# A row-softmax with relative position bias: loads and stores alternating on one queue, in larger chunks, with a written-out order

## The chip, the cores and the metric

The kernel runs on one core of one Trainium2 chip. The metric is the device time of one execution in microseconds (us), as the median of several runs. All runs compared here are of the fast state, except one, which is marked. Times of the kernel before agree within about 0.1%. The sets of experiments ran on three chips, with the kernel before run anew in each set (medians of 1334.1 to 1334.5 us), so a few tenths of a microsecond between sets say nothing.

## The reference

For each of 16 matrices (2 batches, 8 heads) of 2112 x 2112 float32 logits, a bias that depends only on the clipped distance between row and column is added, and each row goes through a softmax:

```python
rel = clip(pos[:, None] - pos[None, :], -16, 16) + 16
logits = logits + rel_bias[:, rel]
logits = logits - logits.max(axis=-1, keepdims=True)
exp = np.exp(logits)
return exp / exp.sum(axis=-1, keepdims=True)
```

Input and output together are 571 MB. Every byte of the input is read once and every byte of the output written once, so this is mostly a copy with arithmetic on the way. (Neither kernel subtracts the row maximum.)

## The kernel before

VectorE, ScalarE, GpSimd and SyncE are engines of the core; the profile calls them DVE, ACT, POOL and SP. Here the last three issue transfers, each into a queue of its own, and the core's 16 DMA engines carry them out. PEclk in the tables belongs to an engine that is not used here.

A partition holds 33 consecutive rows of one head, so 128 partitions hold two heads. A chunk is 3 rows of every partition, 25,344 contiguous bytes per partition. A chunk is loaded, gets the bias added by VectorE in one instruction (`F` is a strip that holds the bias row once, read at a shifted offset for each row), goes through the exponential on ScalarE with the row sums as a by-product, is multiplied by the reciprocal on VectorE, and is stored from the same buffer.

```python
R = 3
io = ctx.enter_context(tc.tile_pool(name="io", bufs=7))
...
def load(c, eng):
    k, row, j, r = c
    L = io.tile([P, R * S], FP32, tag="L", name="L")
    eng.dma_start(out=L[:, 0 : r * S], in_=rows(logits, row, j, r))
    return L

NPRE = 2
pre = [load(c, nc.sync) for c in chunks[:NPRE]]
...
for n, c in enumerate(chunks):
    ...
    L = pre[n] if n < NPRE else load(c, nc.gpsimd)       # loads: GpSimd's queue
    ...
    nc.vector.tensor_tensor(out=L3, in0=L3, in1=F3, op=ALU.add)
    for i in range(r):
        x = L[:, i * S : (i + 1) * S]
        nc.scalar.activation(out=x, in_=x, func=EXP, accum_out=tot[:, i : i + 1])
    nc.vector.reciprocal(out=tot[:, 0:r], in_=tot[:, 0:r])
    for i in range(r):
        x = L[:, i * S : (i + 1) * S]
        nc.vector.tensor_scalar_mul(out=x, in0=x, scalar1=tot[:, i : i + 1])
    nc.sync.dma_start(out=rows(out, row, j, r), in_=L[:, 0 : r * S])   # stores: SyncE's queue
```

A scheduler decides in which order each engine runs these instructions. Loads (after the first two) are issued by GpSimd and stores by SyncE, so two DMA queues are at work.

The softmax here doesn't subtract the row's maximum and nothing guards it: scores larger than these inputs give would overflow.

Of the kernel before, what the change touches and what calls it, by code (L numbers as in the profile page):

```python
# [1 line left out]

# [4 lines left out]

FP32 = mybir.dt.float32
EXP = mybir.ActivationFunctionType.Exp
ALU = mybir.AluOpType  # L10


@with_exitstack
def kernel(
    ctx: ExitStack,
    tc: tile.TileContext,
    logits: bass.AP,
    rel_bias: bass.AP,
    out: bass.AP,
):  # L20




    nc = tc.nc
    P = 128
    B, H, S, S2 = logits.shape
    assert S == S2
    MR = 16
    W = 2 * MR + 1  # L30
    NB = S // W
    assert NB * W == S and 2 * NB == P and H % 2 == 0
    R = 3
    FW = S + W - 1

    const = ctx.enter_context(tc.tile_pool(name="const", bufs=1))
    fpool = ctx.enter_context(tc.tile_pool(name="fpool", bufs=2))
    io = ctx.enter_context(tc.tile_pool(name="io", bufs=7))
    small = ctx.enter_context(tc.tile_pool(name="small", bufs=8))

    chunks = []
    for k in range(H // 2):
        for b in range(B):
            last = k == H // 2 - 1 and b == B - 1
            sizes = [R] * (W // R)
            if last:
                sizes = sizes[:-1] + [1] * R
            j = 0
            for r in sizes:
                chunks.append((k, (b * H + 2 * k) * S, j, r))  # L50
                j += r
            assert j == W

    def rows(t, row, j, r):
        return bass.AP(
            tensor=t.tensor,
            offset=t.offset + (row + j) * S,
            ap=[[W * S, P], [1, r * S]],
        )

    def load(c, eng):
        k, row, j, r = c
        L = io.tile([P, R * S], FP32, tag="L", name="L")
        eng.dma_start(out=L[:, 0 : r * S], in_=rows(logits, row, j, r))  # L64
        return L

    NPRE = 2
    pre = [load(c, nc.sync) for c in chunks[:NPRE]]

    rbB = const.tile([P, H // 2, 2, W], FP32, tag="rbB")  # L70
    nc.scalar.dma_start(
        out=rbB,
        in_=bass.AP(tensor=rel_bias.tensor, offset=rel_bias.offset, ap=[[0, P], [1, H * W]]),
    )

    qm = const.tile([P, NB], FP32, tag="qm")
    for p0 in (0, NB):
        nc.gpsimd.iota(  # L78
            qm[p0 : p0 + NB],
            pattern=[[-1, NB]],  # L80
            base=0,
            channel_multiplier=1,
            allow_small_or_imprecise_dtypes=True,
        )
    eq = const.tile([P, NB], FP32, tag="eq")
    lt = const.tile([P, NB], FP32, tag="lt")
    gt = const.tile([P, NB], FP32, tag="gt")
    for m, op in ((eq, ALU.is_equal), (lt, ALU.is_gt), (gt, ALU.is_lt)):
        nc.vector.tensor_scalar(out=m, in0=qm, scalar1=0.0, scalar2=None, op0=op)  # L89
    rbP = const.tile([P, H // 2, W], FP32, tag="rbP")  # L90
    nc.vector.tensor_copy(out=rbP[0:NB], in_=rbB[0:NB, :, 0, :])  # L91
    nc.vector.tensor_copy(out=rbP[NB:P], in_=rbB[NB:P, :, 1, :])  # L92

    def bias_rows(k):

        F = fpool.tile([P, FW], FP32, tag="F", name="F")
        low = rbP[:, k, W - 1 : W]
        high = rbP[:, k, 0:1]
        rest = small.tile([P, NB], FP32, tag="rest", name="rest", bufs=2)
        nc.vector.tensor_scalar(out=rest, in0=lt, scalar1=low, scalar2=None, op0=ALU.mult)  # L100
        nc.vector.scalar_tensor_tensor(  # L101
            out=rest, in0=gt, scalar=high, in1=rest, op0=ALU.mult, op1=ALU.add
        )
        pitch = list(F.ap[0])[0]
        blocks = bass.AP(
            tensor=F.tensor, offset=F.offset + MR, ap=[[pitch, P], [W, NB], [1, W]]
        )
        rpitch = list(rbP.ap[0])[0]
        rev = bass.AP(
            tensor=rbP.tensor,  # L110
            offset=rbP.offset + k * W + W - 1,
            ap=[[rpitch, P], [0, NB], [-1, W]],
        )

        def wide(t):
            return bass.AP(
                tensor=t.tensor, offset=t.offset, ap=[[list(t.ap[0])[0], P], [1, NB], [0, W]]
            )

        nc.vector.tensor_tensor(out=blocks, in0=wide(eq), in1=rev, op=ALU.mult)  # L120
        nc.vector.tensor_tensor(out=blocks, in0=blocks, in1=wide(rest), op=ALU.add)  # L121
        nc.vector.tensor_copy(out=F[:, 0:MR], in_=low.to_broadcast([P, MR]))  # L122
        nc.vector.tensor_copy(out=F[:, FW - MR : FW], in_=high.to_broadcast([P, MR]))  # L123
        return F

    F, fk = None, None
    for n, c in enumerate(chunks):
        k, row, j, r = c
        if k != fk:
            F, fk = bias_rows(k), k  # L130
        L = pre[n] if n < NPRE else load(c, nc.gpsimd)
        pitch = list(L.ap[0])[0]
        L3 = bass.AP(tensor=L.tensor, offset=L.offset, ap=[[pitch, P], [S, r], [1, S]])

        F3 = bass.AP(
            tensor=F.tensor,
            offset=F.offset + W - 1 - j,
            ap=[[list(F.ap[0])[0], P], [-1, r], [1, S]],
        )
        nc.vector.tensor_tensor(out=L3, in0=L3, in1=F3, op=ALU.add)  # L140
        tot = small.tile([P, R], FP32, tag="tot", name="tot")
        for i in range(r):
            x = L[:, i * S : (i + 1) * S]
            nc.scalar.activation(out=x, in_=x, func=EXP, accum_out=tot[:, i : i + 1])  # L144
        nc.vector.reciprocal(out=tot[:, 0:r], in_=tot[:, 0:r])  # L145
        for i in range(r):
            x = L[:, i * S : (i + 1) * S]
            nc.vector.tensor_scalar_mul(out=x, in0=x, scalar1=tot[:, i : i + 1])  # L148
        nc.sync.dma_start(out=rows(out, row, j, r), in_=L[:, 0 : r * S])


# [1 line left out]
_INS = ['logits', 'rel_bias']  # L153
_OUTS = [((2, 8, 2112, 2112), 'float32')]


# [23 lines left out]
```

## Time and profile before

The median was 1334.06 us (1333.6 to 1334.38, three runs), the span of the profiled execution 1332.3 us.

| what | before |
|---|---|
| bytes moved | 571.19 MB |
| VectorE, ScalarE busy | 71%, 39% |
| DMA between 400 and 800 us | share 1.00, 432 GB/s |
| rbB landed, first add, first store issued | 17.9, 26.4, 57.0 us |

From the page of the kernel before: the span, one line of busy time, the two DMA rows over 40 slices, the packets, and the two queues with the share of the 16 DMA engines' time that their packets took.

```profile
span 1332.3 us, 1666 instructions
...
DVE 947.2 (71%) x473; ACT 524.9 (39%) x529; POOL 49.0 (4%) x94
...
DMA  9999999999999999999999999999999999999998
GB/s 392 415 402 432 432 435 431 434 431 434 431 434 430 434 431 433 432 432 434 432 434 430 434 432 433 432 434 431 433 434 432 432 432 434 431 432 432 433 428 372
DMA packets 26076, 571.19 MB, mean 429 GB/s; under 512 B 2896, under 2 KB 3024, under 8 KB 3024
...
q1 hardware_dynamic: 13248, 291.97, 51.0%
q0 software_dynamic: 12672, 278.99, 48.8%
```

The DMA engines are busy from end to end and everything else waits for them. Only the first three slices and the last two are below the plateau.

The table by stretches, for the kernel before: each line is a stretch, its length, the busy time of each engine, the clock, the DMA share and GB/s.

```profile
core 0: us, DVE busy (x) ACT busy (x) POOL busy (x), PEclk, DMA share, GB/s
30.00:110.00 80.00, 78.44 (x34) 47.59 (x48) 2.11 (x4) 1.00 0.99 415
110.00:190.00 80.00, 57.06 (x30) 33.30 (x33) 2.63 (x5) 1.00 1.00 431
190.00:270.00 80.00, 53.28 (x28) 32.13 (x34) 2.64 (x5) 1.00 1.01 433
270.00:400.00 130.00, 96.37 (x47) 51.05 (x51) 5.43 (x9) 1.00 1.00 433
400.00:800.00 400.00, 283.01 (x140) 157.11 (x160) 13.71 (x26) 1.00 1.00 432
```

After 110 us the kernel before runs at its plateau. Before that it loses rate. One cause is a microsecond in which nothing was queued; in a finer table of the same kernel (the same columns, two lines of it):

```profile
56.00:57.00 1.00, 1.00 (x2) 1.00 (x1) 0.00 (x0) 1.00 0.01 0
57.00:58.00 1.00, 1.00 (x1) 1.00 (x3) 0.00 (x0) 1.00 0.89 380
```

All seven buffers had been loaded and no store had been issued. The timeline of SyncE (start, length, what was issued) shows why:

```profile
start us, us, engine line op out<-in xcount [idle before <-releaser]
0.74 0.86 SPq L64 DMA_DIRECT2D L<-in_logits_dram  x2
57.02 57.79 SPq L149 DMA_DIRECT2D out_dram<-L  x7
```

The scheduler had VectorE run adds, from 26.4 to 53.2 us, before the scales that the first store needs. The start as a whole was late, since the bias table `rbB` shared the engines with the packets of two loading queues; VectorE's waits for the kernel before say so (total, count, longest):

```profile
DVE L L140 <- DMA L<-in_logits_dram: 346.6, 77, 8.2
DVE rbP L91 <- DMA rbB<-in_rel_bias_dram: 17.9, 1, 17.9
```

### The profile page before, as it was taken

The numbers are of one execution on the slowest core, as the hardware profiler recorded it, in microseconds if no ns is written. First come the engines' busy times: TensorE is split into PE (matmuls) and PEld (weight loads), VectorE is DVE, ScalarE is ACT, GpSimd is POOL, SyncE is SP. The second block draws the span as 40 slices with busy tenths as digits, with TensorE's granted clock in tenths as the row PEclk, the third lists the DMA queues.
The fourth block names the chain that finished last, engine by engine and source line by source line (L and its number), as shares of the span: only waits on it lengthen the run. The fifth ranks groups of instructions, "written<-read, shape, count | busy, mean of one in ns | idle before, by whom it ended". The sixth has DMA issues, their size and how long they took to land.

```text
span 1332.3 us, 1666 instructions
## 1 busy us (share of the span) xinstructions
DVE 947.2 (71%) x473; ACT 524.9 (39%) x529; POOL 49.0 (4%) x94
## 2 busy tenths in 40 slices
DVE  4997677669676677767966677766796677766773
ACT  0754334433344333443344333443334333443341
POOL 0000000000000000000000000000000000000000
DMA  9999999999999999999999999999999999999998
GB/s 392 415 402 432 432 435 431 434 431 434 431 434 430 434 431 433 432 432 434 432 434 430 434 432 433 432 434 431 433 434 432 432 432 434 431 432 432 433 428 372
DMA packets 26076, 571.19 MB, mean 429 GB/s; under 512 B 2896, under 2 KB 3024, under 8 KB 3024
## 3 DMA queue, kind: packets, MB, share of 16 engines
q1 hardware_dynamic: 13248, 291.97, 51.0%
q0 software_dynamic: 12672, 278.99, 48.8%
q10 hardware_dynamic: 144, 0.14, 0.0%
q14 instruction: 12, 0.10, 0.0%
HBM read 285.61 MB, written 285.47 MB: 429 GB/s over the span
## 4 chain that ended last, share of the span: by engine, by line
DMA 79%; DVE 11%; issue 7%; another core or an unknown queue 1%; ACT 0%; POOLq 0%; POOL 0%; ACTq 0%
DMA out_dram<-L 47%; DMA L<-in_logits_dram 30%; DVE L L148 6%; DVE L L140 4%; DMA rbB<-in_rel_bias_dram 1%; DVE F L121 0%; DVE F L120 0%; ACT L L144 0%; DVE tot L145 0%; POOLq L64 0%; POOL L L64 0%; DVE rest L100 0%; DVE rest L101 0%; DVE rbP L92 0%
## 5 line engine op out<-in xcount | busy, mean ns | idle before, releaser
L140 DVE TENSOR_TENSOR L<-L,F 128x6336 f32<-128x6336 f32 (+1 forms) x90 | 594.7, 6609 | 346.8 <-DMA L<-in_logits_dram 346.6
L144 ACT ACTIVATE L<-L 128x2112 f32<-128x2112 f32 x264 | 515.2, 1952 | 768.7 <-DVE L L140 756.5
L148 DVE TENSOR_SCALAR L<-L,tot 128x2112 f32<-128x2112 f32 x264 | 331.8, 1313 | 0.0
L64 POOL DMA_DIRECT2D L<-in_logits_dram x88 | 48.5, 551 | 1241.2 <-DMA out_dram<-L 1231.6
L144 ACT ACTIVATION_READ_ACCUMULATOR L<-L 128x1 f32 x264 | 49.2, 186 | 0.0
L145 DVE RECIPROCAL tot<-tot 128x3 f32<-128x3 f32 (+1 forms) x90 | 14.8, 167 | 0.9 <-ACT L L144 0.9
L91 DVE COPY rbP<-rbB 64x132 f32<-64x132 f32 x1 | 0.2, 223 | 17.9 <-DMA rbB<-in_rel_bias_dram 17.9
L121 DVE TENSOR_TENSOR F<-F,rest 128x2112 f32<-128x2112 f32 x4 | 9.4, 2344 | 0.0
L120 DVE TENSOR_TENSOR F<-eq,rbP 128x2112 f32<-128x2112 f32 x4 | 9.4, 2344 | 0.0
L144 ACT ACT_TABLE_LOAD x1 | 1.3, 1283 | 17.8 <-DMA L<-in_logits_dram 17.8
L101 DVE SCALAR_TENSOR_TENSOR rest<-gt,rbP,rest 128x64 f32<-128x64 f32 x4 | 1.0, 265 | 0.0
L100 DVE TENSOR_SCALAR rest<-lt,rbP 128x64 f32<-128x64 f32 x4 | 0.9, 240 | 0.0
L122 DVE COPY F<-rbP 128x16 f32<-128x16 f32 x4 | 0.7, 163 | 0.0
L123 DVE COPY F<-rbP 128x16 f32<-128x16 f32 x4 | 0.7, 167 | 0.0
L78 POOL IOTA qm<- 64x64 f32 x2 | 0.4, 176 | 0.4 <-PEq L175 0.4
L92 DVE COPY rbP<-rbB 64x132 f32<-64x132 f32 x1 | 0.2, 225 | 0.0
L89 DVE TENSOR_SCALAR lt<-qm 128x64 f32<-128x64 f32 x1 | 0.2, 186 | 0.0
L89 DVE TENSOR_SCALAR gt<-qm 128x64 f32<-128x64 f32 x1 | 0.2, 186 | 0.0
L89 DVE TENSOR_SCALAR eq<-qm 128x64 f32<-128x64 f32 x1 | 0.2, 185 | 0.0
L164 POOL MEMSET const-float32-0.0<- 128x1 f32 x1 | 0.1, 98 | 0.2 <-issue 0.2
L164 POOL MEMSET const-bfloat16-1.0<- 128x1 bf16 x1 | 0.1, 101 | 0.0
L164 POOL MEMSET const-float32-1.0<- 128x1 f32 x1 | 0.1, 98 | 0.0
(1 smaller groups left out, 0.1 us busy)
## 6 DMA issues: line engine op xcount, KB each, us to landing
out_dram<-L SPq DMA_DIRECT2D x87, 3168.0 KB, 38.2
L<-in_logits_dram POOLq DMA_DIRECT2D x85, 3168.0 KB, 25.7
L<-in_logits_dram SPq DMA_DIRECT2D x2, 3168.0 KB, 24.3
L<-in_logits_dram POOLq DMA_DIRECT2D x3, 1056.0 KB, 17.0
out_dram<-L SPq DMA_DIRECT2D x3, 1056.0 KB, 18.3
rbB<-in_rel_bias_dram ACTq DMA_DIRECT2D x1, 132.0 KB, 17.2
```

The lines of the kernel that those rows point to most:

```text
L64: eng.dma_start(out=L[:, 0 : r * S], in_=rows(logits, row, j, r))
L89: nc.vector.tensor_scalar(out=m, in0=qm, scalar1=0.0, scalar2=None, op0=op)
L100: nc.vector.tensor_scalar(out=rest, in0=lt, scalar1=low, scalar2=None, op0=ALU.mult)
L101: nc.vector.scalar_tensor_tensor(out=rest, in0=gt, scalar=high, in1=rest, op0=ALU.mult, op1=ALU.add)
L120: nc.vector.tensor_tensor(out=blocks, in0=wide(eq), in1=rev, op=ALU.mult)
L121: nc.vector.tensor_tensor(out=blocks, in0=blocks, in1=wide(rest), op=ALU.add)
L122: nc.vector.tensor_copy(out=F[:, 0:MR], in_=low.to_broadcast([P, MR]))
L123: nc.vector.tensor_copy(out=F[:, FW - MR : FW], in_=high.to_broadcast([P, MR]))
L140: nc.vector.tensor_tensor(out=L3, in0=L3, in1=F3, op=ALU.add)
L144: nc.scalar.activation(out=x, in_=x, func=EXP, accum_out=tot[:, i : i + 1])
L145: nc.vector.reciprocal(out=tot[:, 0:r], in_=tot[:, 0:r])
L148: nc.vector.tensor_scalar_mul(out=x, in0=x, scalar1=tot[:, i : i + 1])
```

## The change

The intent: one SyncE queue carries loads and stores in a fixed alternating order, so that GpSimd has nothing to issue; chunks of 5 and 6 rows, so that there are fewer and longer packets; small first and last chunks, so that compute starts early and ends soon; and the order of every engine's instructions is the order in which they are written (`manual_schedule`). The last scale of a chunk stands behind the first add of the next one. The diff, cut to its core:

```diff
+    SLOT = (5, 6)
-    io = ctx.enter_context(tc.tile_pool(name="io", bufs=7))
+    io = ctx.enter_context(tc.tile_pool(name="io", bufs=2))      # per slot size: 2 + 2 buffers
+    ctx.enter_context(tc.manual_schedule())
-            sizes = [R] * (W // R)
+            sizes = [5, 6] * 3
+            if not chunks:
+                sizes = [1, 2, 3, 5, 5, 6, 5, 6]
+            if k == H // 2 - 1 and b == B - 1:
+                sizes = [5, 6, 5, 6, 5, 3, 2, 1]
+    def load(n):
+        size, r = SLOT[n % 2], chunks[n][3]
+        L[n] = io.tile([P, size * S], FP32, tag=f"L{size}", name="L")
+        nc.sync.dma_start(out=L[n][:, 0 : r * S], in_=rows(logits, n))
+    def store(n):
+        nc.sync.dma_start(out=rows(out, n), in_=L[n][:, 0 : chunks[n][3] * S])
     ...
+    for n in range(4):
+        load(n)
     ...
+    def scale(n, s0, w, tot):
+        ...                                    # reciprocal and w row scales
+        if s0 + w == chunks[n][3]:
+            if n >= 2 and n + 2 < N:
+                load(n + 2)
+            store(n)
     ...
+        for s0 in range(0, r, R):
+            w = min(R, r - s0)
+            add(n, s0, w)
+            cur = (n, s0, w, exps(n, s0, w))
+            if prev:
+                scale(*prev)
+            prev = cur
```

The bias strip of the next pair of heads is built in three steps, one per chunk, instead of at once. The arithmetic is the same.

More of the change, by code (lines that the diff above doesn't have):

```diff
@@ L43 @@
         for b in range(B):
-            last = k == H // 2 - 1 and b == B - 1
-            sizes = [R] * (W // R)
-            if last:
-                sizes = sizes[:-1] + [1] * R
+            sizes = [5, 6] * 3
[3 more added lines that the diff above has]
+                sizes = [5, 6, 5, 6, 5, 3, 2, 1]
             j = 0
@@ L52, with rows @@
             assert j == W
-    def rows(t, row, j, r):
+    N = len(chunks)
+    def rows(t, n):
+        k, row, j, r = chunks[n]
         return bass.AP(
@@ L59, in rows @@
         )
-    def load(c, eng):
-        k, row, j, r = c
-        L = io.tile([P, R * S], FP32, tag="L", name="L")
-        eng.dma_start(out=L[:, 0 : r * S], in_=rows(logits, row, j, r))
-        return L
-    NPRE = 2
-    pre = [load(c, nc.sync) for c in chunks[:NPRE]]
+    L = {}
+    def load(n):
+        size, r = SLOT[n % 2], chunks[n][3]
+        assert r <= size
+        L[n] = io.tile([P, size * S], FP32, tag=f"L{size}", name="L")
+        nc.sync.dma_start(out=L[n][:, 0 : r * S], in_=rows(logits, n))
+    def store(n):
+        nc.sync.dma_start(out=rows(out, n), in_=L[n][:, 0 : chunks[n][3] * S])
     rbB = const.tile([P, H // 2, 2, W], FP32, tag="rbB")
@@ L99, in bias_rows @@
         rest = small.tile([P, NB], FP32, tag="rest", name="rest", bufs=2)
-        nc.vector.tensor_scalar(out=rest, in0=lt, scalar1=low, scalar2=None, op0=ALU.mult)
-        nc.vector.scalar_tensor_tensor(
-            out=rest, in0=gt, scalar=high, in1=rest, op0=ALU.mult, op1=ALU.add
-        )
         pitch = list(F.ap[0])[0]
@@ L118, in wide, with ends @@
             )
-        nc.vector.tensor_tensor(out=blocks, in0=wide(eq), in1=rev, op=ALU.mult)
-        nc.vector.tensor_tensor(out=blocks, in0=blocks, in1=wide(rest), op=ALU.add)
-        nc.vector.tensor_copy(out=F[:, 0:MR], in_=low.to_broadcast([P, MR]))
-        nc.vector.tensor_copy(out=F[:, FW - MR : FW], in_=high.to_broadcast([P, MR]))
-        return F
-    F, fk = None, None
-    for n, c in enumerate(chunks):
-        k, row, j, r = c
-        if k != fk:
-            F, fk = bias_rows(k), k
-        L = pre[n] if n < NPRE else load(c, nc.gpsimd)
-        pitch = list(L.ap[0])[0]
-        L3 = bass.AP(tensor=L.tensor, offset=L.offset, ap=[[pitch, P], [S, r], [1, S]])
+        def ends():
+            nc.vector.tensor_scalar(out=rest, in0=lt, scalar1=low, scalar2=None, op0=ALU.mult)
+            nc.vector.tensor_copy(out=F[:, 0:MR], in_=low.to_broadcast([P, MR]))
+            nc.vector.scalar_tensor_tensor(
+                out=rest, in0=gt, scalar=high, in1=rest, op0=ALU.mult, op1=ALU.add
+            )
+            nc.vector.tensor_copy(out=F[:, FW - MR : FW], in_=high.to_broadcast([P, MR]))
@@ new lines, in band, with fill, add @@
+        def band():
+            nc.vector.tensor_tensor(out=blocks, in0=wide(eq), in1=rev, op=ALU.mult)
+        def fill():
+            nc.vector.tensor_tensor(out=blocks, in0=blocks, in1=wide(rest), op=ALU.add)
+        return F, [ends, band, fill]
+    strips = {}
+    F, steps = bias_rows(0)
+    strips[0] = F
+    for step in steps:
+        step()
+    def add(n, s0, w):
+        k, row, j, r = chunks[n]
+        F, x = strips[k], L[n]
+        x3 = bass.AP(
+            tensor=x.tensor,
+            offset=x.offset + s0 * S,
+            ap=[[list(x.ap[0])[0], P], [S, w], [1, S]],
+        )
@@ L135, with exps @@
         F3 = bass.AP(
             tensor=F.tensor,
-            offset=F.offset + W - 1 - j,
-            ap=[[list(F.ap[0])[0], P], [-1, r], [1, S]],
-        )
-        nc.vector.tensor_tensor(out=L3, in0=L3, in1=F3, op=ALU.add)
+            offset=F.offset + W - 1 - j - s0,
+            ap=[[list(F.ap[0])[0], P], [-1, w], [1, S]],
+        )
+        nc.vector.tensor_tensor(out=x3, in0=x3, in1=F3, op=ALU.add)
+    def exps(n, s0, w):
         tot = small.tile([P, R], FP32, tag="tot", name="tot")
-        for i in range(r):
-            x = L[:, i * S : (i + 1) * S]
+        for i in range(w):
+            x = L[n][:, (s0 + i) * S : (s0 + i + 1) * S]
@@ L144 @@
             nc.scalar.activation(out=x, in_=x, func=EXP, accum_out=tot[:, i : i + 1])
-        nc.vector.reciprocal(out=tot[:, 0:r], in_=tot[:, 0:r])
-        for i in range(r):
-            x = L[:, i * S : (i + 1) * S]
-            nc.vector.tensor_scalar_mul(out=x, in0=x, scalar1=tot[:, i : i + 1])
-        nc.sync.dma_start(out=rows(out, row, j, r), in_=L[:, 0 : r * S])
+        return tot
+    def scale(n, s0, w, tot):
+        nc.vector.reciprocal(out=tot[:, 0:w], in_=tot[:, 0:w])
+        for i in range(w):
+            x = L[n][:, (s0 + i) * S : (s0 + i + 1) * S]
+            nc.vector.tensor_scalar_mul(out=x, in0=x, scalar1=tot[:, i : i + 1])
+        if s0 + w == chunks[n][3]:
+            if n >= 2 and n + 2 < N:
+                load(n + 2)
+            store(n)
@@ new lines @@
+    todo = []
+    prev = None
+    for n, (k, row, j, r) in enumerate(chunks):
+        if k + 1 < H // 2 and k + 1 not in strips and n + 4 < N and chunks[n + 4][0] == k + 1:
+            strips[k + 1], todo = bias_rows(k + 1)
+        for s0 in range(0, r, R):
[5 more added lines that the diff above has]
+            prev = cur
+        if todo:
+            todo.pop(0)()
+    scale(*prev)
```

## The prediction

> **What bounds it now.** The DMA engines. The page moves 571.19 MB in a span of 1332.3 us; its DMA row reads 9 in 39 of 40 slices, and the stretch table from 200 to 1200 us gives 432 GB/s at a DMA share of 1.00. VectorE is busy 71%, ScalarE 39%: neither limits. The Trainium skill (DMA: Bandwidth & Descriptors, "Where 436 GB/s comes from") states a ceiling of 435.2 GB/s; the trace agrees: its DMA records show 25,344-byte packets at 940 ns, 8,448-byte ones at 319 ns, semaphore packets at 9 ns. The line through the two sizes is 27.2 GB/s per engine (435 over 16) plus 8.5 ns per packet.
>
> So the span is, per engine: 1311.6 us of bytes; 1440 packets x 8.5 ns = 12.2; 181 semaphore packets, 1.6; rbB 0.4; about 2 before the first packet; about 4 by which packets overran their usual time, nearly all in the first 80 us, where two queues load together; 1.3 of an idle gap near 57 us (the first store is issued only then: five adds and six scales run ahead of it); and an uneven end, where about 3 of 16 engines finish 3 us after the rest.
>
> **What the change does.**
> 1. The bytes stay: 1311.6 us. This alone rules out a gain over 2% (1307 us).
> 2. Chunks of 5.5 rows instead of 3: data packets per engine fall from 1440 to 832, worth 608 x 8.5 ns = 5.2 us; DMAs from 180 to 104, 0.7 us. Both on the critical path, since the engines never rest.
> 3. The start. First loads of 1, 2 and 3 rows; rbB's packets now alternate with packets of 0.3 and 0.6 us, not two queues' of 0.94, so rbB should land near 7 us, not 17.9, and the first add start near 13 us, not 26.4. The first store should be issued near 21 us, before the four loads (11 rows, about 28 us) are through. No idle gap: 1.3 us, and perhaps 2.5 of the overruns.
> 4. The end: one queue, engines even: 1 to 2 us.
> 5. Fixed order: the last scale of chunk n stands behind the first add of chunk n+1, which waits for its load. The store of n is issued about 11 us after load n+1 lands (add 6.6, reciprocal, three scales of 1.3), while the queue still holds the store of n-1 and the load of n+2, about 27 us. Loads wait for a store that landed two transfers back. So the queue should never run dry. DVE's waits change but cost nothing.
> 6. Direction changes inside one queue: before, engines alternated load and store packets of two queues without a gap, so I charge nothing.
>
> **Sum.** 1334.1 - 5.9 - 3.8 - 1.5 = 1323; built from the floor, 2 + 1319.6 + 0.4 + 1.2 after the last packet + 1.9 outside the span = 1325. I predict 1326 us, 8 in 10 between 1322 and 1334. Faster by over 2%: 1%; same: 96%; slower: 3%.
>
> **What would show it.** Plateau near 433.5 GB/s; packets of 42,240 bytes at 1561 ns and 50,688 at 1872; about 15,000 packets; one hardware queue with 99%; first store near 21 us; no slice of the DMA row under 9 but the ends.
>
> **What would make it wrong.** A pause at each load-to-store change in one queue: 104 times 0.3 us would be 31 us. Larger packets split by the hardware would lose step 2. A late store letting the queue run dry once per chunk would cost several per cent.

## The result, and the profile after

The changed kernel takes 1332.38 us (median of six, 1331.58 to 1332.98) against 1334.14 us (1333.6 to 1334.38). The ratio is 0.9987, with a 95% interval of 0.9974 to 1.0: 1.8 us faster in the medians, where 8 were forecast. The interval reaches 1.0, so the gain is small against the noise, though each of the six runs was below each of the six of the kernel before. Ratios here are the mean time of one kernel's fast runs over that of the other's of the same rounds, so they are not quite the ratios of the medians quoted. Profiled runs: the changed kernel's took 1331.58 us, the fastest of its runs, which matters below. The outputs are right.

From the page of the changed kernel, the lines that answer to those of before:

```profile
span 1329.8 us, 1414 instructions
...
DVE 955.0 (72%) x489; ACT 525.8 (40%) x529; POOL 0.6 (0%) x6
...
DMA  9999999999999999999999999999999999999998
GB/s 386 431 422 428 425 429 435 430 434 429 432 435 433 434 432 429 436 436 430 437 429 437 434 428 441 426 436 433 430 441 424 441 428 437 428 432 437 431 425 378
DMA packets 15130, 571.17 MB, mean 430 GB/s; under 512 B 1680, under 2 KB 1808, under 8 KB 1808
...
q1 hardware_dynamic: 14976, 570.96, 99.8%
```

One queue, 15,130 packets, DMA at 9 nearly throughout: as forecast. The start came out as forecast too. From the changed kernel's SyncE timeline, and from VectorE's waits:

```profile
0.74 2.05 SPq L73 DMA_DIRECT2D L<-in_logits_dram  x4
21.48 9.67 SPq L76 DMA_DIRECT2D out_dram<-L  x2
```

```profile
DVE L L163 <- DMA L<-in_logits_dram: 354.9, 49, 10.7
DVE rbP L102 <- DMA rbB<-in_rel_bias_dram: 5.7, 1, 5.7
```

The first store was issued at 21.5 us, not 57, and the empty microsecond is gone. Now the same table by stretches, for the changed kernel:

```profile
core 0: us, DVE busy (x) ACT busy (x) POOL busy (x), PEclk, DMA share, GB/s
30.00:110.00 80.00, 64.72 (x32) 36.44 (x39) 0.00 (x0) 1.00 1.00 422
110.00:190.00 80.00, 52.83 (x28) 31.25 (x32) 0.00 (x0) 1.00 1.00 429
190.00:270.00 80.00, 59.26 (x33) 33.74 (x34) 0.00 (x0) 1.00 1.00 431
270.00:400.00 130.00, 98.96 (x49) 53.57 (x54) 0.00 (x0) 1.00 1.00 434
400.00:800.00 400.00, 284.96 (x142) 153.95 (x156) 0.00 (x0) 1.00 1.00 433
```

The DMA share is 1.00 in every line, so no engine stood idle, and yet only 422 to 431 GB/s moved until 270 us. The engines were busy with packets that took longer than usual. That is the first thing to explain. The second is the plateau: 433 against 432, for chunks nearly twice as long.

### Where the time went, packet by packet

The trace lists every DMA packet with start, length and size. Nearly all packets of a size have the same length: 319 ns for 8,448 bytes, 629 for 16,896, 940 for 25,344, 1561 for 42,240, 1872 for 50,688, 9 for a semaphore packet. I call what a packet takes beyond the usual length of its size its overrun, and give the sum over all packets divided by 16, that is, per engine. The ring of each of the 16 engines ends a transfer with a semaphore packet, so the 16 times at which a transfer ends show how far apart the engines are. The profiled runs of both kernels, from the first data packet to the last:

| us, per engine | before | changed | difference | forecast |
|---|---|---|---|---|
| undisturbed transfer of 528 row-loads and row-stores | 1319.6 | 1316.7 | -2.9 | -5.9 |
| overruns | 4.2 | 7.1 | +2.9 | -2.5 |
| nothing queued near 57 us | 1.3 | 0 | -1.3 | -1.3 |
| the rest: engines that finish late | 4.1 | 3.0 | -1.1 | -1.5 |
| first packet to last | 1329.2 | 1326.8 | -2.4 | |

The first line is worked out from the distance between successive ends of transfers on the earliest engine in the steady part, per row and direction: 2.4992 us before and 2.4938 us after, times 528. The last but one line is a remainder.

Two terms of the forecast are off, by 3.0 and 5.4 us; together that is more than the whole miss of 6.4 us. The experiments test both.

The overruns of the changed kernel after the start fall almost wholly on loads that stand between stores. The load that ended near 76 us and the one that ended near 102 us overran by 0.7 us per engine each; after 450 us only two of 33 loads overran by over 0.1 (0.19 and 0.29). Meanwhile the engines had drifted apart: they ended a transfer within 0.7 us of each other at 32 us, 2.1 at 101 us, and 4.8 at 400 us.

### The profile page after: what moved, and what is told of

Its sections match the earlier page's. It is cut to its first block, busy times and chain, and to the rows that moved or that the text cites. A ratio compares the mean times of both kernels' runs of the same rounds, so it can differ in the third digit from the quotient of the medians.

```text
span 1329.8 us, 1414 instructions
## 1 busy us (share of the span) xinstructions
DVE 955.0 (72%) x489; ACT 525.8 (40%) x529; POOL 0.6 (0%) x6
## 2 busy tenths in 40 slices
DMA packets 15130, 571.17 MB, mean 430 GB/s; under 512 B 1680, under 2 KB 1808, under 8 KB 1808
## 4 chain that ended last, share of the span: by engine, by line
DMA 85%; DVE 14%; issue 0%; SPq 0%; DVEq 0%
DMA L<-in_logits_dram 49%; DMA out_dram<-L 36%; DVE L L163 9%; DVE L L176 4%; DMA rbB<-in_rel_bias_dram 0%; DVE F L139 0%; DVE F L136 0%; DVE tot L173 0%; SPq L76 0%; DVEq L163 0%; DVE rest L128 0%; DVE rest L130 0%; DVE rbP L103 0%; DVE rbP L102 0%; DVE F L133 0%
## 5 line engine op out<-in xcount | busy, mean ns | idle before, releaser
L163 DVE TENSOR_TENSOR L<-L,F 128x4224 f32<-128x4224 f32 (+2 forms) x98 | 596.0, 6082 | 354.9 <-DMA L<-in_logits_dram 354.9
L173 DVE RECIPROCAL tot<-tot 128x2 f32<-128x2 f32 (+2 forms) x98 | 16.3, 166 | 0.0
```

The lines of the kernel that those rows point to most:

```text
L163: nc.vector.tensor_tensor(out=x3, in0=x3, in1=F3, op=ALU.add)
L173: nc.vector.reciprocal(out=tot[:, 0:w], in_=tot[:, 0:w])
```

## The experiments

Theory A: packets overrun where all 16 engines change between loads and stores together. One queue in a fixed order forces this at every change, until the engines have drifted apart; two queues that mix packet by packet avoid it. The expectations speak of the change from stores to loads, and of a load's first packets, because I had seen only that the overruns lay in loads. That detail was wrong: a closer count (experiment 5) puts three quarters of them there on a load's last packet, just before the next store. Its rivals are named in the expectations: chance (B), the larger packets themselves (C), the hole near the end (D), late stores (F), the early part of the run (G).

Overruns per engine in us, by part of the run, from the trace of each experiment; "apart" is the distance between the first and the last engine at the end of a transfer near 105 us.

| kernel | median us | 0-30 us | 30-110 | 110-270 | 270-end | apart, us |
|---|---|---|---|---|---|---|
| before | 1334.1 | 1.6 | 2.2 | 0.0 | 0.3 | 0.8 |
| changed | 1332.4 | 1.6 | 2.1 | 1.5 | 1.9 | 2.1 |
| changed, again | 1333.0 | 1.7 | 2.6 | 1.3 | 1.9 | 3.4 |
| scale moved forward at the end | 1333.2 | 1.7 | 2.7 | 1.8 | 2.8 | 2.2 |
| transfers alone | 1331.5 | 1.5 | 2.2 | 1.0 | 0.9 | 2.5 |
| 3 rows, one queue | 1335.7 | 1.5 | 2.6 | 1.3 | 1.0 | 2.6 |
| 5 and 6 rows, loads on GpSimd | 1352.6 | 1.6 | 1.0 | 1.3 | 12.6 | 3.1 |
| first load cut | 1334.4 | 4.6 | 1.8 | 0.3 | 1.6 | 3.4 |
| second load cut | 1342.8 | 11.2 | 2.0 | 0.2 | 1.2 | 3.3 |
| 3 rows, loads on GpSimd | 1332.7 | 1.7 | 1.5 | 0.1 | 0.4 | 3.5 |
| 4 rows, loads on GpSimd | 1341.0 | 1.7 | 2.3 | 0.3 | 15.8 | 3.1 |
| 3 rows, stores on ScalarE | 1330.8 | 1.6 | 0.1 | 0.1 | 0.4 | 0.8 |

### 1. The changed kernel again (no edit)

> The changed kernel unchanged, for a second trace. In its first trace the packets took their predicted times (nominal sum 1320.4 us per engine against 1326.1 before), but packets overran that time by 7.1 us per engine (4.2 before), and from 30 us on nearly all of the overrun fell on the first packets of a load that follows a store. Theory A (a store-to-load change costs up to 0.7 us while the 16 engines change in step, until they have drifted about 4 to 5 us apart): the same pattern again, 3 to 6 us of overrun after 30 us, engines 4 to 6 us apart by 400 us, time 1331.5 to 1333. Theory B (chance in one trace): overrun after 30 us under 2 us or spread evenly over the span.

Measured: 1332.97 us (1332.62 to 1333.97), ratio 0.999. The pattern is the same, with 5.8 us of overrun after 30 us and engines 4.9 us apart at 400 us. Chance (B) is out. This profiled run took 1333.97 us, 2.4 us longer than the first, so the changed kernel's time scatters more than that of the kernel before, and the gain in the first trace (2.7 us) is flattering. The medians are the better numbers.

### 2. Loads on GpSimd's queue, chunks of 5 and 6 rows

```diff
-        nc.sync.dma_start(out=L[n][:, 0 : r * S], in_=rows(logits, n))
+        eng = nc.sync if n < 4 else nc.gpsimd
+        eng.dma_start(out=L[n][:, 0 : r * S], in_=rows(logits, n))
```

> The changed kernel, with every load after the first four issued from GpSimd's queue instead of SyncE's: chunks of 5 and 6 rows, buffers and engine order stay, but loads and stores can mix packet by packet again. Theory A (the loss is the store-to-load change of all engines in step, which one queue in fixed order forces): the overrun after the first 120 us goes to under 1 us as before, the nominal 1320.4 us stay, and the time is 1327 to 1330 us. Theory C (the larger packets overrun by themselves): the overrun stays near 7 us and the time near 1332.

Measured: 1352.64 us, ratio 1.0135. Both expectations missed; the overrun after 120 us was 13.7 us per engine. Three lines of this run's stretch table have the reason in them (columns as above):

```profile
560.00:640.00 80.00, 58.29 (x34) 30.44 (x32) 3.35 (x3) 1.00 1.01 433
1100.00:1180.00 80.00, 54.53 (x27) 32.23 (x34) 3.90 (x3) 1.00 1.01 425
1280.00:1290.00 10.00, 9.96 (x6) 5.20 (x5) 0.00 (x0) 1.00 0.50 212
```

In the first stretch both queues had packets in flight most of the time, and the rate is the plateau. Then two of the 16 engines fell behind, to 13 and 15 us near 790 us. With only four buffers every load waits for a whole store to land, so for those two engines. By 1100 us the two queues no longer mixed: in the trace the packets of one queue filled 94% of the time for 10 us and more, then those of the other, and the fourteen engines in step overran at each change (the second line, 425 GB/s). Twice near the end fourteen engines stood idle, for about 7 and 5 us, until the two had caught up (the third line shows the first time). Two queues are thus no cure by themselves. It looks as if the buffers must be enough to keep both supplied; experiments 10 and 11 bear on that. That the engines fell behind is shown; why those two is not.

### 3. Chunks of 3 rows in one queue

```diff
-    SLOT = (5, 6)
+    BUFS = 7
-            sizes = [5, 6] * 3
+            sizes = [R] * 11
-                sizes = [1, 2, 3, 5, 5, 6, 5, 6]
+                sizes = [1, 2] + [R] * 10
-                sizes = [5, 6, 5, 6, 5, 3, 2, 1]
+                sizes = [R] * 10 + [2, 1]
-            if n >= 2 and n + 2 < N:
-                load(n + 2)
+            if n >= 2 and n + BUFS - 2 < N:
+                load(n + BUFS - 2)
```

> The changed kernel with chunks of 3 rows in 7 buffers (as before), but one SyncE queue in fixed order. Nominal packet sum near 1326 us again. Theory A: overruns of 3 to 6 us at store-to-load changes until the engines stand several us apart, time 1335 to 1339 us, slower than before. Theory C (large packets are what overruns): overruns as before, 4 us or less, time 1332.5 to 1334.5 us, since the idle gap of the start is gone.

Measured: 1335.74 us (1334.07 to 1336.93), ratio 1.0009. The overruns after 30 us are 4.8 us, nearly those of the large chunks, and fall on the same part of the run. The larger packets (C) are not their cause; one queue is enough. Only the chunks and their buffers differ, so this run also prices them, though roughly: 1335.74 - 1332.97 = 2.8 us, with runs that scatter by 2.9 us, where the forecast had 5.9 us.

### 4. The scale moved forward at the end

In the changed kernel's trace the DMA share sinks near the end. The stretch table of the changed kernel:

```profile
1316.00:1318.00 2.00, 1.97 (x4) 1.66 (x1) 0.00 (x0) 1.00 0.68 291
1318.00:1320.00 2.00, 1.96 (x3) 0.40 (x2) 0.00 (x0) 1.00 0.59 253
1320.00:1322.00 2.00, 0.35 (x1) 0.00 (x0) 0.00 (x0) 1.00 0.96 401
```

The store of 2 rows stood behind the add of the last row, which waited for its load. This is the one place where the fixed order let the queue run dry, contrary to step 5 of the forecast. The edit puts the scale first:

```diff
+            if n >= N - 2 and prev:
+                scale(*prev)
+                prev = None
             add(n, s0, w)
```

> The changed kernel, with the last two chunks' scales moved ahead of the adds of the chunk after them, so that the store of 2 rows no longer waits for the load of the last row. In the changed kernel's trace the engines are idle 1.5 us on the mean near 1317 to 1320 us, because that store comes late. Theory D (this hole costs its 1.5 us): time 1.2 to 1.6 us lower than the changed kernel. Theory E (the slowest of the 16 engines sets the end and had no hole: it finished the store before at 1321.7 us, after the late store was issued at 1318.95): the hole goes from the trace but the time changes by less than 0.4 us.

Measured: 1333.23 us (1332.52 to 1333.62), against 1332.97 us for the changed kernel on the same chip. The hole is gone, as the stretch table of this run shows, and the time has not moved:

```profile
1316.00:1320.00 4.00, 2.32 (x1) 1.59 (x1) 0.00 (x0) 1.00 0.98 422
```

The times alone do not exclude theory D, since this run's overruns were also 1.5 us higher than those of the repeat, as much as D's gain. The traces decide for theory E: in the changed kernel the four engines that ended last, at 1327.7 to 1328.5 us, had no gap between packets after 1290 us, while ten of the others waited, up to 3.7 us, for the late store. So the hole only made the early engines wait: with it all 16 ended the run within 1.1 us of each other, without it (in this run) within 4.7 us.

### 5. The transfers alone

The adds, exponentials and scales are taken out; each store sends back what its load brought, in the same queue and order. The output is wrong.

```diff
-        for s0 in range(0, r, R):
-            ...                      # add, exps, scale of the piece before
+        if n >= 2 and n + 2 < N:
+            load(n + 2)
+        store(n)
-    scale(*prev)
```

> Wrong output on purpose: the changed kernel's 104 transfers in the same queue and order, without the adds, exponentials and scales (each store sends back what its load brought). If the time of the changed kernel is all DMA (theory A), the time stays at 1331 to 1334 us and the overrun after 30 us stays at 4 to 6 us per engine, at loads that follow stores. If late stores and VectorE's fixed order matter (theory F), it falls by 2 us or more.

Measured: 1331.48 us (1330.37 to 1332.15), ratio 0.9979. All the arithmetic together costs the changed kernel 1 to 1.5 us, and 4.2 us of overrun after 30 us remain without it. Late stores and VectorE's order (F) explain at most 1.5 us of the miss of 6.4.

In this trace every packet can be assigned to its place in its transfer, since each engine goes through the same 936 packets and nearly always starts one 3 to 4 ns before the record of the one before it ends. Of the 4.2 us per engine after 30 us, 3.1 fall on the last of the eight packets of a load, the one before a store, 0.5 on the first three packets of a load, and hardly any on stores. Sorted the same way, the changed kernel's two traces have 3.8 of 5.5 us and 3.1 of 5.8 us on that packet; with the shorter packets of experiment 3, 2.5 of 4.8 us fall on the last but one and 0.9 on the last. So it is the end of a load, just before a store, that overruns. Some of the loads, with how far apart the engines ended them:

| load of chunk | ends near, us | overrun of its last packet, us per engine | engines apart, us |
|---|---|---|---|
| 4 | 53 | 0.40 | 0.9 |
| 5 | 76 | 0.61 | 1.5 |
| 6 | 102 | 0.61 | 2.5 |
| 7 | 130 | 0.27 | 3.1 |
| 8 | 157 | 0.14 | 3.3 |
| 11 | 241 | 0.28 | 4.5 |
| 13 | 296 | 0.03 | 4.5 |
| 14 | 324 | 0.15 | 5.5 |
| 18 | 434 | 0.00 | 5.8 |
| 31 | 790 | 0.00 | 5.7 |

While all engines turn from a load to a store within a packet's time (1.6 to 1.9 us) or little more, each loses up to 0.6 us on the mean; those that lose more fall behind; and once they are spread over nearly 6 us nothing is lost any more. The decline is not even (0.28 us are lost at 4.5 us apart, 0.03 at the same distance later), so the distance is not the whole account.

### 6 and 7. Engines set apart on purpose

The first load (then instead the second) is cut into transfers of 48, 55 and 25 partitions. The Trainium skill (DMA: Bandwidth & Descriptors, "Why a DMA increments its semaphore by 16 and not by 1") says that a transfer runs on the largest number of engines up to 16 that divides its slowest dimension. The trace agrees: the cut adds 16 semaphore packets, which is what 16, 11 and 5 engines instead of 16 make.

```diff
-        nc.sync.dma_start(out=L[n][:, 0 : r * S], in_=rows(logits, n))
+        cuts = (0, 48, 103, P) if n == 0 else (0, P)        # n == 1 in the second run
+        for p0, p1 in zip(cuts, cuts[1:]):
+            nc.sync.dma_start(out=L[n][p0:p1, 0 : r * S], in_=rows(logits, n, p0, p1))
```

> The changed kernel with the first load (1 row) cut into three transfers of 48, 55 and 25 partitions. If a transfer spreads over as many engines as divide its partitions, up to 16, five engines get 13 packets, six get 8 and five get 3, so that three groups of engines stand 1.6 us apart (3.2 us in all) before the first store, and the last group ends 1.6 us after the mean for it. Theory A (the overrun comes from engines that change from stores to loads together): overrun after 30 us falls from 5.4 to 5.8 us per engine to between 1.5 and 3.5; time 1330 to 1333. Theory G (the overrun belongs to the early part of the run or to each change as such, whatever the engines' distance): it stays at 5 to 6 us, and the time is 1.6 us higher, near 1334.

> The same cut made in the second load (2 rows) instead: groups 3.1 us apart, 6.3 us in all, the last group 3.1 us behind the mean. Theory A: overrun after 30 us under 1.5 us; time within 1330 to 1333, since the stagger costs about what it saves. Theory G: overrun 5 to 6 us, time near 1335.5.

Measured: 1334.42 us (ratio 1.0002) and 1342.79 us (ratio 1.0067). The cut transfers themselves overran, by 3 and by 9.6 us per engine more than an uncut start, which I had not reckoned with and which makes the second time useless. Nor did three groups form; at 60 us eleven engines stood together and five about 1.8 us (2.8 us in the second run) behind. What the runs do show is the stretch from 110 to 270 us: overruns of 0.3 and 0.2 us, against 1.5 and 1.3 in the two traces of the changed kernel. Over all that follows 30 us they come to 3.7 and 3.4 us, against 5.5 and 5.8; theory A had asked for at most 3.5 and 1.5, so its size was missed. Setting the engines apart lessens the overruns at the same time of the run, which G does not allow. But from 30 to 110 us, with eleven engines still together, it saved little (1.8 and 2.0 us against 2.1 and 2.6). It is support, not proof, and no way to win time.

### 8. Loads on ScalarE's queue

```diff
+        eng = nc.sync if n < 4 else nc.scalar
+        eng.dma_start(out=L[n][:, 0 : r * S], in_=rows(logits, n))
```

> The changed kernel with the loads after the first four issued from ScalarE's queue. The run with GpSimd's queue was slower (1352.6 us): two of 16 engines fell 13 to 18 us behind on GpSimd's loads between 550 and 800 us. Theory H (that is due to GpSimd's queue alone): here no engine falls more than 6 us behind and the time is 1329 to 1333 us. Theory I (two queues with only four buffers do this whatever issues the loads): two engines fall behind again, time over 1340 us.

Measured: 1684.85 us, ratio 1.2633. Neither theory foresaw this. ScalarE now reaches the instruction that issues a load only after exponentials that wait for VectorE, which waits for the load before. Every chunk ends in a hole in which no engine has work, as two lines of this run's stretch table show:

```profile
764.00:768.00 4.00, 3.94 (x1) 0.00 (x0) 0.00 (x0) 1.00 0.39 169
768.00:772.00 4.00, 3.96 (x3) 1.09 (x1) 0.00 (x0) 1.00 0.00 0
```

The holes add to 267 us of idle time per engine between the first and last packet. As a by-product the run is the clearest view of the overruns. Each hole sets the 16 engines back in step (half of the loads, over the whole run, end within 1.3 us on all engines). The load whose packets start at 772.0 to 772.6 us starts on all 16 engines from idle: its first packets overrun by 0.8 us on the mean, after 5 us without any packet. Its third packets, those just before the first packets of a store on each engine, overrun by 0.9 to 1.4 us on all 16, 1.2 on the mean. After that load and store packets alternate on every engine, still nearly in step, and of 209 packets only two overrun, by 0.11 and 0.14 us. The same comes back with every chunk, 2 to 3.6 us in each 40 us, at 1600 us as at 100. So a change of direction as such costs nothing here; a change that all engines make together, out of a stretch of loads, does. Time alone does not make it fade; that it fades in the changed kernel fits the drift of the engines there.

### 9. Transfers alone, one row each

```diff
-    SLOT = (5, 6)
+    BUFS = 22
-            sizes = [5, 6] * 3
+            sizes = [1] * 33
```

> Wrong output on purpose: the transfers alone, in one queue and fixed order, in chunks of one row and 22 buffers. Against the transfers alone of the changed kernel (1331.5 us; 832 data packets and 104 semaphore packets per engine) it has 4224 and 528: 3816 more. Theory P (a packet costs about 5 ns beyond its bytes, as the distance between successive landings in the steady stretch says: 2.499 us per row and direction with chunks of 3, 2.493 with 5 and 6, where the bytes take 2.485): 3816 x 5 ns = 19 us more, about 1350. Theory Q (8.5 ns, as the packet records' lengths say and the prediction took): 32 us more, about 1364.

Measured: 1409.08 to 1440.91 us, 1434.73 in the middle of four, three of the four (the profiled one among them) slow, so the time tells nothing for certain. It is swamped by 87 us of overruns: here every engine changes between loads and stores every 2.5 us, and the engines stay within 4 us of each other. But the trace has quiet stretches with next to no overrun, and there the distance of successive ends answers the question. It is 2.528 us per row and direction, with 8 data packets and a semaphore packet in it. The bytes take 67,584 / 27.2 GB/s = 2.485 us, so a packet costs (2.528 - 2.485) / 9 = 4.8 ns. Theory Q asked for 2.562. In bytes, theory P asks for 427 GB/s and Q for 422; the stretch table of this run, in a quiet part, and its queue line:

```profile
720.00:800.00 80.00, 0.00 (x0) 0.00 (x0) 1.00 1.01 427
```

```profile
q1 hardware_dynamic: 76032, 570.98, 100.4%
```

The second line gives the flaw away. Packets of one queue cannot fill 100.4% of the engines' time unless their records overlap. The usual lengths that I had read contain some 3 to 4 ns that belong to the next packet too, which is by how much an engine's records overlap in the trace of experiment 5.

### 10. Chunks of 3 rows, two queues (loads on GpSimd)

This is experiment 3 with the edit of experiment 2: the kernel before with the changed kernel's start and order.

> Chunks of 3 rows in 7 buffers, fixed order, first loads of 1 and 2 rows, loads after the first four from GpSimd's queue: the kernel before with the changed kernel's start and order. Theory A (overruns come where the engines start loads together; with seven buffers the two queues stay mixed): overrun after 40 us under 1.5 us per engine, no engine more than 5 us behind, time 1331 to 1333.5 us, faster than 3 rows in one queue (1335.7) by 2 to 4 us. If two queues fall into alternation here too: overrun 4 us or more and 1335 us or more.

Measured: 1332.70 us (1332.52 to 1332.79), ratio 0.9989. With seven buffers the queues stay mixed and the overruns after 110 us are 0.5 us. It is 3.0 us faster than the same chunks in one queue, and as fast as the changed kernel. The overrun after 40 us was about 2 us, above the 1.5 expected; it fell between 30 and 110 us, and one engine ended 6 us behind the median of its stores, not 5.

### 11. Chunks of 4 rows in 5 buffers, two queues (loads on GpSimd)

```diff
-    BUFS = 7
+    BUFS, C = 5, 4
-            sizes = [R] * 11
+            sizes = [C] * 7 + [3, 2]
-        size, r = R, chunks[n][3]
+        size, r = C, chunks[n][3]
```

> The same with chunks of 4 rows in 5 buffers. Theory A with the smaller cost of a packet: 1.3 us less than chunks of 3 rows if the queues stay mixed, 1330 to 1332 us. If five buffers are too few to keep loads and stores mixed, engines fall behind as with four buffers (1352.6 us): 1336 us or more.

Measured: 1340.99 us, but anywhere from 1335.33 to 1354.45 in six runs; ratio 1.0064. In the profiled run (1354.45 us) three engines fell 13 us and more behind, as two did in experiment 2. Five buffers of 4 rows are too few here. The buffers hold nearly as many rows in all as in experiment 10 (20 and 21), so chunk length and number of buffers changed together, and which of the two matters was not tested.

### 12. Chunks of 3 rows, loads on SyncE and stores on ScalarE

One edit to experiment 3. ScalarE reaches the store after the exponentials of the next chunk, which itself wait for VectorE, so the store adds no wait for what would otherwise run.

```diff
-        nc.sync.dma_start(out=rows(out, n), in_=L[n][:, 0 : chunks[n][3] * S])
+        nc.scalar.dma_start(out=rows(out, n), in_=L[n][:, 0 : chunks[n][3] * S])
```

> Chunks of 3 rows in 7 buffers and fixed order; loads on SyncE's queue, stores on ScalarE's, issued where ScalarE would wait for VectorE's scale anyway. Two queues without GpSimd. Theory A (the two queues mix, so engines do not start loads together): overrun after 70 us under 1 us per engine. Theory H (engines that fall steadily behind belong to GpSimd's queue): no engine more than 3 us behind the median at 1250 us (2.5 to 6 us in the run of 3 rows with GpSimd's loads). Both together: 1329.5 to 1331.5 us, faster than both kernels by 1 us or more. If the time is 1332.5 or more, one of them is wrong.

Measured: 1330.76 us (1330.53 to 1330.96), ratio 0.9972, interval 0.9958 to 0.9986: the fastest correct kernel, 3.7 us below the kernel before in the same rounds. From the stretch tables, first of experiment 3, then of this run (columns as above):

```profile
30.00:110.00 80.00, 74.61 (x36) 44.01 (x47) 0.00 (x0) 1.00 1.01 419
110.00:190.00 80.00, 53.12 (x25) 31.49 (x32) 0.00 (x0) 1.00 1.00 426
190.00:270.00 80.00, 57.68 (x30) 29.74 (x30) 0.00 (x0) 1.00 1.01 433
```

```profile
30.00:110.00 80.00, 64.45 (x31) 40.02 (x42) 0.00 (x0) 1.00 1.00 432
110.00:190.00 80.00, 55.58 (x26) 29.76 (x30) 0.00 (x0) 1.00 1.01 433
190.00:270.00 80.00, 58.17 (x28) 30.46 (x31) 0.00 (x0) 1.00 1.00 432
```

In this run the plateau is there from 30 us on. Against experiment 3, where only the queue of the stores differs, the overruns after 30 us go from 4.8 to 0.5 us and the time from 1335.7 to 1330.8 us. The queues do mix: in every stretch of 5 us from 50 to 1290 us the loads' queue has between 0.34 and 0.62 of the packets' time. And the engines stand as close together as in the kernel before (0.8 us apart near 105 us), so it is the mixing that avoids the overruns, not distance. For this kernel, then, one queue costs about 4 to 5 us, and two queues that stay mixed cost almost none of it. One thing moves along with the queue: in experiment 3 SyncE held a finished store back while the load before it waited for its buffer, and here it does not, so the times of issue change too (the eighth load at 35.7 us, not 52.5). Theory H is half refuted: three engines fell behind, by 2.9, 3.3 and 3.8 us at 1250 us, with GpSimd's queue not in use at all, so the small lag is not GpSimd's; the large ones (13 us and more) were seen only with GpSimd's loads and few buffers.

## Why the prediction was right or wrong

- **What bounds the kernel, and that no gain over 2% was possible: right.** The DMA share stayed at 1.00, and with no arithmetic at all the time was 1331.5 us.
- **Step 2, larger chunks worth 5.9 us: the mechanism right, the size wrong.** The packets fell from 26,076 to 15,130 and took 1561 and 1872 ns, as forecast. But the cost of a packet, 8.5 ns, came from the lengths of packet records, and these overlap. It measures 4.8 ns (experiment 9), and 608 data packets and 76 semaphore packets fewer are 684 x 4.8 = 3.3 us by that figure. The distances of landings say 2.9 us, and experiments 1 and 3 say 2.8, roughly. The profile had shown it: 25,344 bytes in 940 ns on 16 engines are 431.4 GB/s, and the tables said 432 to 433 with a share of up to 1.01.
- **Step 3, the start: the events right, half of the gain wrong.** The first store came at 21.5 us (forecast 21), the first add at 13.2 (13), rbB at 7.3 (7), and the 1.3 us gap went. The 2.5 us of overruns did not go: those of the first 30 us are the same (1.6 us), and those of 30 to 110 us too (2.2 and 2.1), since the old ones were replaced by the new. A price for start and order alone: experiment 10, which keeps the chunks and the two queues of the kernel before, was 1.4 us faster than it (1332.70 against 1334.13), where this step had 3.8.
- **Step 4, a more even end worth 1 to 2 us: near in the table (1.1 us), but by luck.** The 1.1 us are a remainder. Read from the traces, the engines ended 2.8 us before the last one on the mean in the kernel before, and 0.9 us in the changed one; but there they had also waited 1.5 us on the mean for the late store, so the gain at the end is about 0.4 us. The reason given, even engines, did not hold: they had drifted 4.7 us apart, and only that wait drew them together.
- **Step 5, the queue never runs dry: right but for one place**, the store of 2 rows near the end, which cost no time that experiment 4 could find.
- **Step 6, "so I charge nothing" for direction changes in one queue: wrong, and the larger part of the miss.** The reason given was that two queues alternate load and store packets without a gap. That says nothing of a queue that turns all engines from loads to stores together. The overruns rose by 2.9 us in the profiled pair, where a fall of 2.5 was forecast. The closing section had named this risk at 0.3 us for each of 104 changes. In the two traces of the changed kernel it is 0.4 to 1.0 us for each of the first three loads between stores and 0 to 0.4 us for the later ones.

In sum, the forecast's terms came to -11.2 us, from which it kept some distance at -8.1. Measured were -2.9 for the packets, +2.9 for the overruns, -1.3 for the gap and -1.1 for the end: -2.4 us in the profiled pair, and -1.8 in the medians. What stays open is what holds the end of a load when all engines turn to stores together, and why it is always a few engines that fall behind in the mixed queues. Nor was the larger chunk tried with the stores on ScalarE, where the saving of step 2 might have come without the overruns.

## What to carry to other kernels

A kernel at a DMA share of 1.00 can still lose rate: compare GB/s by stretch, not only the share, and look at what the packets of slow stretches have in common. Two queues that stay mixed gave a steadier stream than one queue in strict alternation, but here only with seven buffers of 3 rows, not with five of 4 or four of 5 and 6; a queue on a compute engine is free only where that engine would wait anyway. And take the price of a packet from the distance between landings, not from the length of its record.

## What the Trainium skill lacked or had wrong

- DMA: Bandwidth & Descriptors, "Issuing engines are not separate DMA queues", says that starting DMAs from several engines only saves issue time. Here 3-row chunks took 1335.7 us with loads and stores in one SyncE queue and 1330.8 us with the stores in ScalarE's (experiments 3 and 12); the page lacks that one queue makes all engines change direction together, and that this cost about 4 to 5 us of overruns. Another page, Perfetto Trace Analysis, "DMA Optimizations", does advise one engine for inputs and another for outputs, but for another reason and without a number.
- DMA: Bandwidth & Descriptors, "Latency and other measured facts", says that some engines are usually slower and guesses at GpSimd's descriptors as the cause. Three of 16 engines fell 2.9 to 3.8 us behind with no GpSimd transfer in the kernel (experiment 12), so that guess does not cover this lag; with GpSimd's loads and few buffers it reached 13 us and more (experiments 2 and 11). The trace does not name the engines.
- The same page, "Why small descriptors are slow (HBM only)", gives about 3 cycles of overhead per packet. If they are cycles of the 850 MHz in "Where 436 GB/s comes from", that would be about 3.5 ns, an estimate; the quiet stretches of experiment 9 measure 4.8 ns. The ceiling of 435.2 GB/s in that section agrees with the bytes' rate read here (27.2 GB/s per engine).
- No page says that the lengths of DMA packet records overlap, so that they overstate what a packet costs: a queue line read 100.4% of the engines' time, and 8.5 ns from records were 4.8 ns by landings (experiment 9).
